# Decoder layer with retention and top-256 sparse attention: a 272-key threshold read from the smallest end, 784 keys counted on another engine, shorter mask passes, retention outputs kept in PSUM

## The chip, the cores and the metric

The program runs on one core of one Trainium2 chip. The metric is the device time of one execution in microseconds (us), taken as the median of several runs. Beside the runs there is one profiled execution, whose trace gives every instruction's start and length on the five queues of the core: TensorE (PE, with its weight loads listed as PEld), VectorE (DVE), ScalarE (ACT), GpSimd (POOL) and SyncE (SP), which issues the DMAs.

## The reference, cut to what matters

One decoder layer on 1024 tokens with 16 meta tokens in front (so 1040 keys at most), model width 1024. Two token mixers work side by side on the same normed input; their outputs are joined, projected, and an MLP follows.

```
# A) retention: 4 heads of 128, in chunks of 128 tokens, state S carried from chunk to chunk
scores  = (q_c k_c^T) * decay_mask           # within the chunk
o       = scores v_c + (q_c * xi) S          # xi = exp(log_gamma*(i+1)) per row i and head
y_ret   = silu(g) * rmsnorm(o, gain)         # norm over the head's 128 columns, EPS 1e-6

# B) sparse attention: per query an index score for every causal key, the best 256 kept
score   = sum_h iw_h * relu(iq_h . ik)       # NEG where not causal
_, sel  = lax.top_k(score, 256)              # ties: the lower key index first
p       = softmax(q . k[sel] + t5_bias)      # 8 heads of 64, one shared k and v
y_dsa   = p v[sel]

h = h + concat(y_ret, y_dsa) @ w_out
h = h + square(relu(rmsnorm(h) @ w_ff1)) @ w_ff2
```

The kernel does not gather. For each block of 128 queries it finds the 256th largest score of every row, makes a row of 0 and 1e30 from it (0 for a kept key) and adds that to the logits.

## The kernel before, in words

The 1024 queries are 8 tiles of 128; query tile i sees `ncol[i]` = 16 + 128(i+1) keys, so 144, 272, 400, 528, 656, 784, 912 and 1040. Tile 0 needs no choice (144 keys are fewer than 256). Large products run as three passes in float32r: each operand is split into a rounded high half (ACT) and a remainder (POOL or DVE).

The stages follow one another on TensorE, with the other engines' work for the next stage laid between:

1. The first norm and the index: for each tile, small projections, the index queries (`index_q`) and the index scores (`index`: two matmuls per head and key range, a Relu on ACT, a multiply-add on DVE into `sc[i]`).
2. The query projection of the attention (tensor `qn`), then retention. For each of 4 heads: `ret_meta` (the 16 meta tokens give the first state), then 8 chunks, 32 chunks in all. `ret_in` projects one chunk into one PSUM buffer of 128x512 (24 matmuls of 512 columns) and reads q, k, v and the gate out of it: DVE multiplies by cos and sin (`t`, lines 437 and 438), ACT makes `vz` and `th`, DVE `gs` and `fg`. Three such buffers (`psA`) exist, so TensorE can be at most three projections ahead. `ret_out`, one chunk later, transposes q and k, forms scores `sm` (DVE), the output `p2` (PE) and the next state `S` (DVE). ACT copies the output scaled by the row factor into `oh` (line 501) and squares it with a sum (line 502). After every fourth chunk DVE multiplies `oh` by the norm's factor and `fg` (line 506), and a DMA stores it to `yrd`.
3. The threshold search `topk` belongs to no TensorE stage: it runs on DVE and ACT while TensorE does stages 1 and 2. It is a bisection over the 31 bits of the float's pattern, a round per bit. Tiles 2, 3, 4 and 5 (400, 528, 656, 784 keys) are one group: DVE counts the scores at or above the candidate in one pass per tile (line 713), then two small instructions give the next candidate. Tiles 1, 6 and 7 (272, 912, 1040 keys) are the other: ACT counts with a Sign activation and a sum (line 718), DVE turns each tile's count into a bit (line 744) and makes the next candidate (line 752), on which ACT's next round waits. Then each tile's mask is made by DVE (lines 771 to 779): a count of greater scores, the places of equal ones, a running sum over these, two combining passes and a last one that writes `sc[i]`.
4. Attention: units of one query tile and four heads (`attend_p`, `attend_v`), mixed with the output projection (`out_piece`, whose weights `load_cols` splits on ACT, POOL and DVE).
5. Second norm, MLP in a Strassen-like form; from 725 us on.

The SBUF of stages 1 to 3 (pool `p1`, named `big`) is given back as a whole before stage 4's pool `p2` takes the same bytes. The tile `pm` (the probabilities of the meta keys) is allotted in `p2` and set to zero by DVE (line 795) before its first use; so that memset waits for the last user of the bytes it takes, among them the store of the last `oh`.

The order of the instructions on each engine is not written out: a scheduler places them, before the program runs, by its own estimate of times. On the chip every engine then works through its own list in that order, and waits where an operand isn't ready.

Of the kernel before, what the change touches and what calls it, by code (L numbers as in the profile page):

```python
# [12 lines left out]
I32 = mybir.dt.int32  # L13
# [23 lines left out]
def shape_constants():  # L37
# [44 lines left out]
def layer(ctx, tc, x, meta, norm1_w, w_in, ret_w, q_w, k_w, rel, w_out, norm2_w, w1, w2,  # L82
# [52 lines left out]
    for f in (1.0, 4.0, 64.0):  # L135
# [3 lines left out]
    def rsqrt(ms, k, f=1.0, P=128):  # L139
        y = small.tile([128, k], F32, name="rs_y", tag=f"rsy{k}", bufs=1 if k == 9 else 6)  # L140
        nc.gpsimd.tensor_tensor(y[:P], ms, epst[f][:P, :k], op=ALU.add)
# [43 lines left out]
    def split(raw, n, alt=False):  # L185
# [3 lines left out]
        nc.scalar.activation(shp, raw, AF.Copy)  # L189
        if alt:  # L190
            altc[0] += 1
        (nc.vector if alt and altc[0] % 2 else nc.gpsimd).tensor_tensor(shl, raw, shp.bitcast(F32), op=ALU.subtract)  # L192
        return hi, lo

    def load_cols(src, slices, d0=0, nd=8, alt=False):
        n = sum(w for _, w in slices)
        hs, ls = [], []
        for d in range(d0, d0 + nd, 2):
# [14 lines left out]
            for j in range(2):  # L213
                h, l = split(raw[:, j], n, alt)
# [203 lines left out]
    bias = ap_.tile([128, 8, WIN], F32, name="bias")  # L418
    kr = rsqrt(kss, 9)
# [41 lines left out]
    def ret_in(h, c):  # L461
        hs, ls = st["w", h]
        q = c % 4
        if q == 0:
            st["ss", h] = small.tile([128, 4], F32, name="ssr")
            st["oh", h] = big.tile([128, 4, 128], F32, name="oh", tag="oh", bufs=3)
# [8 lines left out]
        gs = big.tile([128, 128], F32, name="gs", tag="gs", bufs=2)  # L475
        nc.vector.tensor_tensor(gs, ps[:, 384:512], rgain[:, 128 * h:128 * h + 128], op=ALU.mult)  # L476
        nc.vector.scalar_tensor_tensor(st["fg", h][:, q], th, 1.0, gs, op0=ALU.add, op1=ALU.mult)
        return h, c, ro, vz, st["ss", h], st["oh", h], st["fg", h]

    def ret_out(h, c, ro, vz, ssr, oh, fg):  # L480
# [13 lines left out]
        p2 = psB()  # L494
        nc.tensor.matmul(p2[:, 0:128], qkT[:, 0:128], S, start=True, stop=False)
        nc.tensor.matmul(p2[:, 0:128], sm, vz, start=False, stop=True)
# [4 lines left out]
        nc.scalar.activation(oh[:, q], p2[:, 0:128], AF.Copy, scale=vecs[:, 0, h:h + 1])  # L501
        nc.scalar.activation(jk, oh[:, q], AF.Square, scale=2.0 * 128.0 ** -0.5, accum_out=ssr[:, q:q + 1])
        if q == 3:
            r = rsqrt(ssr, 4, 4.0)
            for j in range(4):
                nc.vector.scalar_tensor_tensor(oh[:, j], oh[:, j], r[:, j:j + 1], fg[:, j], op0=ALU.mult, op1=ALU.mult)
# [85 lines left out]
    def attend_v(i, g):  # L592
# [6 lines left out]
        for k, (b, k0, kp) in enumerate(tiles):  # L599
# [8 lines left out]
            if b == 8:  # L608
                ph, pl = at["pm"], at["pm"][ML:]
# [46 lines left out]
    def out_w(ch, alt=False):  # L656
        ow[0] = load_cols(w_out, [(512 * ch, 512)], alt=alt)
# [62 lines left out]

    def topk(g, on_act):
# [451 lines left out]
```

## Time and profile before

| what | us |
|---|---|
| median of 3 runs (1337.89 to 1338.53) | 1338.28 |
| the profiled execution's own time | 1337.21 |
| its span, first to last instruction | 1335.4 |
| PE busy in the span | 1260.4 (94%) |
| DVE busy | 1080.1 (81%) |
| ACT busy | 752.5 (56%) |
| POOL busy | 264.7 (20%) |

The span is cut below at the points where the work changes. "chunks" are retention's; a chunk's end is the end of its projection on PE.

| stretch, us | work on PE | PE busy | DVE busy |
|---|---|---|---|
| 106 to 189 | index tiles 5 to 7, query projection, chunk 1 | 81.52 of 83.00 | 79.67 |
| 189 to 285.7 | chunks 2 to 14 | 89.56 of 96.70 | 93.58 |
| 285.7 to 386.8 | chunks 15 to 27 | 93.46 of 101.10 | 92.50 |
| 386.8 to 438.5 | chunks 28 to 32, first attention unit | 46.08 of 51.70 | 46.49 |
| 438.5 to 453 | the seam into attention | 6.08 of 14.50 | 6.94 |
| 453 to 725 | attention, output projection, second norm | 251.14 of 272.00 | 207.13 |

How to read it: a stretch's length is what counts for the time. A matmul's busy time reaches beyond the start of the next one, since they are pipelined, so PE busy is not what PE needs; the need is the number of matmuls times the distance of their starts where nothing waits. DVE's and ACT's rows overlap a little too (some 80 ns).

### The profile page before, as it was taken

What the parts mean: (1) busy time and instruction counts of PE and PEld (TensorE: products, weight loads), DVE (VectorE), ACT (ScalarE), POOL (GpSimd) and SP (SyncE); (2) the same over time, 40 slices, a digit from 0 to 9 for tenths busy, and PEclk for the clock granted to TensorE, in tenths of its full rate; (3) what the DMA queues carried; (4) which work ended last, traced back from release to release, by engine and by line L of the source; (5) the groups of instructions that cost most, each with busy time, mean ns of one, the idle gap of its engine ahead of it and who ended that gap; (6) DMA issues with size and microseconds to landing.
All of it is one profiled execution on the core that took longest, in us unless ns stands there. A gap on an engine that the chain in (4) does not pass through costs nothing. (4 is left out here: it accounts for less than half of the span.)

```text
span 1335.4 us, 18540 instructions
## 1 busy us (share of the span) xinstructions
PE 1260.4 (94%) x6144; PEld 1044.1 (78%) x6144; DVE 1080.1 (81%) x2395; ACT 752.5 (56%) x1598; POOL 264.7 (20%) x305
## 2 busy tenths in 40 slices
PE   5999999899898699899997999999999999999998
PEld 5888877688687577787775888888887888888887
DVE  5579999999978778677659878777778988887875
ACT  6566657787644567666656545445556444444442
POOL 4003471433526323410244000000000200000000
PEclk8999999899899799999998999999999999999999
DMA  8103040211202111212263444434537844435222
GB/s 276 61 17 90 32 124 17 71 36 50 59 25 71 64 59 37 71 49 79 100 208 103 139 145 144 159 131 151 188 110 286 349 183 159 158 127 189 95 88 102
DMA packets 93664, 153.73 MB, mean 115 GB/s; under 512 B 7240, under 2 KB 47344, under 8 KB 89856
## 3 DMA queue, kind: packets, MB, share of 16 engines
q1 hardware_dynamic: 93568, 152.56, 33.1%
q8 instruction: 48, 0.79, 0.2%
q14 instruction: 48, 0.39, 0.1%
HBM read 110.58 MB, written 43.46 MB: 115 GB/s over the span
## 5 line engine op out<-in xcount | busy, mean ns | idle before, releaser
L924 ACT ACTIVATE wh<-ga 128x512 fp32r<-128x512 f32 x144 | 87.2, 628 | 158.1 <-PE psB L1072 141.4
L242 PE MATMUL psA<-wh,uh 128*128 128x512 f32 x376 | 152.2, 405 | 3.6 <-DVE gs L476 2.0
L243 PE MATMUL psA<-wh,ul 128*128 128x512 f32 x376 | 150.1, 400 | 0.0
L244 PE MATMUL psA<-wl,uh 128*128 128x512 f32 x376 | 149.9, 399 | 0.0
L925 DVE TENSOR_TENSOR wl<-ga,wh 128x512 fp32r<-128x512 f32 x144 | 96.7, 688 | 47.3 <-ACT wh L924 46.8
L924 ACT ACTIVATE wh<-sum 128x512 fp32r<-128x512 f32 x128 | 78.5, 625 | 77.3 <-DVE sum L921 71.2
L1072 PE MATMUL psB<-wh,wl 128*128 128x512 f32 x280 | 109.1, 389 | 0.2 <-DVE wl L925 0.2
L1073 PE MATMUL psB<-wl,wh 128*128 128x512 f32 x280 | 108.9, 389 | 0.0
L1071 PE MATMUL psB<-wh 128*128 128x512 f32 x280 | 106.8, 389 | 0.0
L718 ACT ACTIVATE jk_top<-sc,tcand 128x272 bf16<-128x272 f32 (+2 forms) x93 | 84.9, 913 | 32.0 <-DVE tcand L752 29.9
L713 DVE TENSOR_SCALAR_CACHE_REDUCE jk_cnt<-sc,tcand 128x400 bf16<-128x400 f32 (+1 forms) x124 | 102.1, 823 | 0.8
L925 DVE TENSOR_TENSOR wl<-sum,wh 128x512 fp32r<-128x512 f32 x128 | 87.7, 685 | 5.9 <-ACT wh L924 5.9
L991 POOL COPY ga<-wl 128x1 f32<-128x1 f32 x8 | 6.6, 829 | 404.8 <-DVE wl L925 361.1
L242 PEld LDWEIGHTS psA<-wh,uh 128*128 128x128 f32 x376 | 72.0, 192 | 17.8 <-DVE gs L476 2.6
L244 PEld LDWEIGHTS psA<-wl,uh 128*128 128x128 f32 x376 | 71.9, 191 | 14.7
L243 PEld LDWEIGHTS psA<-wh,ul 128*128 128x128 f32 x376 | 72.2, 192 | 13.1
L192 POOL TENSOR_TENSOR wl<-wr,wh 128x512 fp32r<-128x512 f32 x56 | 78.2, 1413 | 20.3 <-ACT wh L189 13.2
L354 ACT ACTIVATE rl<-psB,absw 128x320 f32<-128x320 f32 (+5 forms) x104 | 52.7, 555 | 33.6 <-PE psB L352 19.9
L611 DVE TENSOR_TENSOR ph<-psB,ph 128x512 fp32r<-128x512 f32 x72 | 49.2, 687 | 20.4 <-ACT ph L610 15.6
L1072 PE MATMUL psA<-wh,wl 128*128 128x512 f32 x168 | 65.4, 389 | 0.0
L1073 PE MATMUL psA<-wl,wh 128*128 128x512 f32 x168 | 65.4, 389 | 0.0
L1071 PE MATMUL psA<-wh 128*128 128x512 f32 x168 | 64.9, 389 | 0.0
(375 smaller groups left out, 3658.2 us busy)
## 6 DMA issues: line engine op xcount, KB each, us to landing
ga<-hid SPq DMA_DIRECT2D x28, 1024.0 KB, 4.9
wr<-in_w_ff_dram SPq DMA_DIRECT2D x34, 512.0 KB, 4.7
hid<-hs SPq DMA_DIRECT2D x48, 256.0 KB, 2.0
wr<-in_w_in_dram SPq DMA_DIRECT2D x32, 256.0 KB, 3.1
gb<-in_w_ff_dram SPq DMA_DIRECT2D x8, 1024.0 KB, 5.0
ga<-in_w_ff_dram SPq DMA_DIRECT2D x8, 1024.0 KB, 5.8
wr<-in_w_out_dram SPq DMA_DIRECT2D x12, 512.0 KB, 4.0
xt<-in_x_dram SPq DMA_DIRECT2D x8, 512.0 KB, 4.5
```

The source lines that it names most:

```text
L192: (nc.vector if alt and altc[0] % 2 else nc.gpsimd).tensor_tensor(shl, raw, shp.bitcast(F32), op=ALU.subtract)
L242: nc.tensor.matmul(ps[:P, :n], uh, wh, start=d == 0, stop=False)
L243: nc.tensor.matmul(ps[:P, :n], ul, wh, start=False, stop=False)
L244: nc.tensor.matmul(ps[:P, :n], uh, wl, start=False, stop=d == 7)
L354: nc.scalar.activation(r[:, :w], ps[:, :w], AF.Relu, scale=absw[:, i, h:h + 1])
L713: nc.vector.tensor_scalar(jk_[:, :ncol[i]], sc[i], cand[:, j:j + 1], 0.0, op0=ALU.is_ge, op1=ALU.add, accum_out=cnt[:, j:j + 1])
L718: nc.scalar.activation(jk_top[:, :ncol[i]], sc[i], AF.Sign, scale=-1.0, bias=cand[:, j:j + 1], accum_out=cnt[:, j:j + 1])
L924: nc.scalar.activation(view(hi), s, AF.Copy)
L925: nc.vector.tensor_tensor(view(lo), s, view(hi).bitcast(F32), op=SUB)
L1071: nc.tensor.matmul(ps[tb], ah[:, t], bh, start=j == 0 and m not in CONT, stop=False, skip_group_check=True)
L1072: nc.tensor.matmul(ps[tb], al[:, t], bh, start=False, stop=False, skip_group_check=True)
L1073: nc.tensor.matmul(ps[tb], ah[:, t], bl, start=False, stop=j == NO - 1, skip_group_check=True)
```

## The change

- `topk`'s group on DVE loses the 784-key tile and keeps 400, 528 and 656; the group on ACT gets it and loses the 272-key tile: 784, 912, 1040. The bits of ACT's group are made for all three tiles at once (against a row of limits `tlim`), and the part of the next candidate that doesn't need the count (`tflip`) is made beforehand.
- The 272-key tile has a routine of its own, `top_few`: the 256th largest of 272 is the 17th smallest, so the scores are negated (ACT), DVE takes the largest eight three times, striking them out twice, and picks one.
- `masks` replaces the passes after the search: ACT counts with Sign, DVE marks the equal scores and counts them in one pass, the running sum and the two combining passes stay on DVE, and ACT writes the last one.
- Retention: the four outputs of a group of chunks stay in one PSUM buffer `p2` (one of the five `psB`); ACT squares them from there and no longer copies them; the row factor moves into the EPS of the norm. The norm's weight `rgain` is no longer multiplied into the gate (`gs` is gone, `fg` reads PSUM) but into the rows of `w_out` that belong to retention: `split` scales ACT's half and takes the remainder with one scalar_tensor_tensor on DVE.
- `pm` is allotted in the attention pool, beside `bias`, and set to zero by POOL early in retention.

The core of the diff:

```
     def split(raw, n, alt=False, gain=None):
-        nc.scalar.activation(shp, raw, AF.Copy)
+        nc.scalar.activation(shp, raw, AF.Copy, scale=1.0 if gain is None else gain)
...
+        else:
+            nc.vector.scalar_tensor_tensor(shl, raw, gain, shp.bitcast(F32), op0=ALU.mult, op1=ALU.subtract)
...
+    pm = ap_.tile([128, 512], F32R, name="pm")
+    nc.gpsimd.memset(pm.bitcast(F32), 0.0)
...
+            st["p2", h] = psB()
...
-        nc.vector.tensor_tensor(gs, ps[:, 384:512], rgain[:, 128 * h:128 * h + 128], op=ALU.mult)
-        nc.vector.scalar_tensor_tensor(st["fg", h][:, q], th, 1.0, gs, op0=ALU.add, op1=ALU.mult)
+        nc.vector.scalar_tensor_tensor(st["fg", h][:, q], th, 1.0, ps[:, 384:512], op0=ALU.add, op1=ALU.mult)
...
-        nc.scalar.activation(oh[:, q], p2[:, 0:128], AF.Copy, scale=vecs[:, 0, h:h + 1])
-        nc.scalar.activation(jk, oh[:, q], AF.Square, scale=2.0 * 128.0 ** -0.5, accum_out=ssr[:, q:q + 1])
+        nc.scalar.activation(jk, po, AF.Square, scale=2.0 * 128.0 ** -0.5, accum_out=ssr[:, q:q + 1])
...
+    def masks(i, T, jk_):
+        nc.scalar.activation(jk_[:, :n], sc[i], AF.Sign, scale=-1.0, bias=T, accum_out=cnt[:, 0:1])
+        nc.vector.tensor_scalar(eq[:, :n], sc[i], T, 0.0, op0=ALU.is_equal, op1=ALU.add, accum_out=cnt[:, 1:2])
...
+        nc.vector.tensor_tensor_scan(cum[:, :n], eq[:, :n], eq[:, :n], 0.0, op0=ALU.add, op1=ALU.max)
+        nc.vector.scalar_tensor_tensor(eq[:, :n], cum[:, :n], need, eq[:, :n], op0=ALU.is_gt, op1=ALU.mult)
+        nc.vector.scalar_tensor_tensor(eq[:, :n], sc[i], T, eq[:, :n], op0=ALU.is_lt, op1=ALU.add)
+        nc.scalar.activation(sc[i], eq[:, :n], AF.Copy, scale=BIG)
...
+    def top_few(i):
+        k = n - TOPK
+        nc.scalar.activation(neg, sc[i], AF.Copy, scale=-1.0)
+        for t in range(k // 8 + 1):
+            nc.vector.max(out=m8, in_=neg)
+            if t < k // 8:
+                nc.vector.match_replace(out=neg, in_to_replace=m8, in_values=neg, imm_value=-3e38)
...
-    runs = [topk([2, 3, 4, 5], False), topk([1, 6, 7], True)]
+    runs = [top_few(1), topk([2, 3, 4], False), topk([5, 6, 7], True)]
...
-    at["pm"] = p2["p"].tile([128, 512], F32R, name="pm")
-    nc.vector.memset(at["pm"].bitcast(F32), 0.0)
```

The order changes with it. Three places matter, all on DVE.

First, index tile 5. The rows begin with the zero count of the 656-key tile (`tz`); `iq` is the index query, `sc` with `rl` the index scores, `wl` the remainder of a weight. Before:

```order
L713 TENSOR_SCALAR jk_cnt,tcnt<-sc,tz 128x656
L342 TENSOR_TENSOR iq<-psB,iq 64x4x128
L192 TENSOR_TENSOR wl<-wr,wh 128x512 x2
L278 COPY kn<-smp 128x64
L284 TENSOR_SCALAR w_119<-smp 128x8
L285 SCALAR_TENSOR_TENSOR absw<-w_119 128x8
L356 TENSOR_SCALAR sc<-rl,sgnw 128x384
```

And now:

```order
L718 TENSOR_SCALAR jk_cnt,tcnt<-sc,tz 128x656
L772 TENSOR_SCALAR tt<-tcnt 128x3
L346 TENSOR_TENSOR iq<-psB,iq 64x4x128
L780 TENSOR_SCALAR tcand<-tt 128x3
L194 TENSOR_TENSOR wl<-wr,wh 128x512
L718 TENSOR_SCALAR jk_cnt,tcnt<-sc,tcand 128x400
L194 TENSOR_TENSOR wl<-wr,wh 128x512
L718 TENSOR_SCALAR jk_cnt,tcnt<-sc,tcand 128x528
L282 COPY kn<-smp 128x64
L288 TENSOR_SCALAR w_117<-smp 128x8
L360 TENSOR_SCALAR sc<-rl,sgnw 128x384
L718 TENSOR_SCALAR jk_cnt,tcnt<-sc,tcand 128x656
```

The group no longer waits for tile 5, so its rounds begin here: 12 rounds of three counts stand ahead of retention's first chunk, where 6 rounds of four (and one count) stood.

Second, chunk 18, from the reading of its projection (`t`) to that of chunk 19. Before:

```order
L437 TENSOR_TENSOR t_3261<-psA,pk 128x256
L438 TENSOR_TENSOR t_3262<-psA,pk 128x256
L744 TENSOR_SCALAR tt<-tcnt 128x1
L713 TENSOR_SCALAR jk_cnt,tcnt<-sc,tcand 128x784
L752 SCALAR_TENSOR_TENSOR tcand<-tcand,tt 128x3
L748 TENSOR_SCALAR tt<-tcnt 128x4
L752 SCALAR_TENSOR_TENSOR tcand<-tcand,tt 128x4
L713 TENSOR_SCALAR jk_cnt,tcnt<-sc,tcand 128x400
L744 TENSOR_SCALAR tt<-tcnt 128x1
```

And now:

```order
L443 TENSOR_TENSOR t_3260<-psA,pk 128x256
L444 TENSOR_TENSOR t_3261<-psA,pk 128x256
L793 SCALAR_TENSOR_TENSOR tcand<-tt,tflip 128x3
L790 TENSOR_SCALAR tflip<-tcand 128x3
L791 TENSOR_TENSOR tt<-tcnt,tlim 128x3
L793 SCALAR_TENSOR_TENSOR tcand<-tt,tflip 128x3
L790 TENSOR_SCALAR tflip<-tcand 128x3
L481 SCALAR_TENSOR_TENSOR fg<-th,psA 128x128
```

DVE's counts ended in chunk 12 and its group's masks in chunk 15; up to chunk 26 only the small instructions of ACT's rounds are left beside retention's own.

Third, the seam, where the last `oh` of retention meets the first `pm`. Before:

```order
L583 TENSOR_REDUCE m_5169<-mn 128x1
L506 SCALAR_TENSOR_TENSOR oh<-oh,rs_y,fg 128x128 x4
L795 MEMSET pm 128x512
L611 TENSOR_TENSOR pm<-psB,pm 16x512 x2
L577 ISA P,mn<-psA,sc 128x32
```

And now:

```order
L592 RECIPROCAL rs<-sums 128x4
L616 TENSOR_TENSOR pm<-psB,pm 16x512
L588 TENSOR_REDUCE m_4968<-mn 128x1
L582 ISA P,mn<-psA,mb 128x240
L582 ISA mn 128x1
L560 TENSOR_TENSOR qs<-psA,qs 64x4x128
L582 ISA P,mn<-psA,sc 128x32
```

The memset is gone from DVE's list and the first `pm` stands ahead of the last `oh`.

## Rows read from the trace of the kernel before

**Rows 1.** Stretches: length, busy us (instructions) per engine, granted clock, DMA share, GB/s.

```profile
60.00:106.00 46.00, 45.11 (x274) 39.01 (x272) 31.99 (x74) 30.95 (x78) 1.56 (x5) 1.00 0.06 19
106.00:189.00 83.00, 81.52 (x392) 68.56 (x391) 79.67 (x156) 51.70 (x101) 44.28 (x39) 0.98 0.26 81
189.00:285.70 96.70, 89.56 (x449) 74.37 (x448) 93.58 (x312) 68.31 (x177) 31.25 (x50) 0.96 0.17 49
285.70:386.80 101.10, 93.46 (x471) 77.38 (x470) 92.50 (x297) 73.60 (x198) 41.35 (x60) 0.95 0.18 50
386.80:438.50 51.70, 46.08 (x254) 39.06 (x253) 46.49 (x125) 23.54 (x83) 29.27 (x32) 0.97 0.21 67
438.50:453.00 14.50, 6.08 (x28) 4.80 (x28) 6.94 (x21) 3.99 (x10) 2.75 (x2) 0.53 0.17 55
...
750.00:800.00 50.00, 50.00 (x222) 41.40 (x221) 39.27 (x64) 25.69 (x47) 0.00 (x0) 1.00 0.48 169
```

**Rows 2.** Timeline of PE at 404 us: start, length, line, tiles, count.

```profile
404.44 0.39 PE L489 MATMUL psB<-qkT 128*128 128x128 f32 x2
404.66 0.39 PE L491 MATMUL psB<-vz,ro 128*128 128x128 f32 x2
```

**Rows 3.** Waits of PE, 195 to 440 us: total, times, longest.

```profile
PE psB L496 <- DVE sm L493: 12.0, 4, 5.1
```

**Rows 4.** Waits of ACT, 195 to 390 us.

```profile
ACT jk_top L718 <- DVE tcand L752: 29.9, 21, 5.2
```

**Rows 5.** Timelines of PE and DVE around chunk 1.

```profile
196.95 0.41 DVE L437 TENSOR_TENSOR t<-psA,pk 128x256 f32<-128x256 f32 x1
...
198.16 1.28 DVE L713 TENSOR_SCALAR_CACHE_REDUCE jk_top<-sc,tz 128x1040 bf16<-128x1040 f32 x1
...
199.38 2.77 DVE L294 SCALAR_TENSOR_TENSOR knl<-psB,knh 64x512 fp32r<-64x512 f32 x4
...
203.30 0.47 PE L242 MATMUL psA<-wh,uh 128*128 128x512 f32 x1 [1.62 <-DVE tt L732]
```

**Rows 6.** DVE's groups by shape, 100 to 440 us: busy us, mean ns, idle.

```profile
L713 DVE TENSOR_SCALAR_CACHE_REDUCE jk_cnt<-sc,tcand 128x784 bf16<-128x784 f32 x31 | 31.7, 1023 | 0.1
L713 DVE TENSOR_SCALAR_CACHE_REDUCE jk_cnt<-sc,tcand 128x656 bf16<-128x656 f32 x31 | 27.6, 889 | 0.0
L713 DVE TENSOR_SCALAR_CACHE_REDUCE jk_cnt<-sc,tcand 128x528 bf16<-128x528 f32 x31 | 23.5, 757 | 0.2
L713 DVE TENSOR_SCALAR_CACHE_REDUCE jk_cnt<-sc,tcand 128x400 bf16<-128x400 f32 x31 | 19.3, 624 | 0.5
L476 DVE TENSOR_TENSOR gs<-psA,rgain 128x128 f32<-128x128 f32 x32 | 9.0, 283 | 1.0 <-ACT th L474 0.8
L499 DVE SCALAR_TENSOR_TENSOR S<-S,psB 128x128 f32<-128x128 f32 x28 | 7.7, 275 | 0.0
L771 DVE TENSOR_SCALAR_CACHE_REDUCE jk_top<-sc,tfin 128x272 bf16<-128x272 f32 x1 | 0.5, 496 | 0.3 <-POOL tfin L764 0.3
```

**Rows 7.** The tile `oh` on DVE, 189 to 440 us: min/median/max ns.

```profile
L506 DVE SCALAR_TENSOR_TENSOR oh<-oh,rs_y,fg x29: 340/348/2271, 238.4 to 439.1; 128x128 f32<-128x128 f32 x29
```

**Rows 8.** ACT's groups by shape, 100 to 440 us.

```profile
L718 ACT ACTIVATE jk_top<-sc,tcand 128x1040 bf16<-128x1040 f32 x31 | 36.0, 1163 | 0.6
L718 ACT ACTIVATE jk_top<-sc,tcand 128x912 bf16<-128x912 f32 x31 | 32.7, 1054 | 0.6
...
L718 ACT ACTIVATE jk_top<-sc,tcand 128x272 bf16<-128x272 f32 x31 | 16.2, 523 | 30.8 <-DVE tcand L752 29.9 <-DVE tcand L737 0.7
...
L501 ACT ACTIVATE oh<-psB,pk 128x128 f32<-128x128 f32 x32 | 11.6, 362 | 23.9 <-PE psB L496 23.6
```

**Rows 9.** The seam: DVE's timeline from 439 us, and PE's waits, 438 to 453.

```profile
439.13 3.06 DVE L506 SCALAR_TENSOR_TENSOR oh<-oh,rs_y,fg 128x128 f32<-128x128 f32 x4
444.60 0.48 DVE L795 MEMSET pm<- 128x512 f32 x1 [2.41 <-issue]
...
PE psB L612 <- DVE pm L611: 8.4, 2, 7.0
```

More of the change, by code (lines that the diff above doesn't have):

```diff
@@ L134, in layer @@
     epst = {}
-    for f in (1.0, 4.0, 64.0):
+    for f in (1.0, 64.0):
         epst[f] = const.tile([128, 9], F32, name=f"eps{int(f)}")
@@ L139, in rsqrt @@
     def rsqrt(ms, k, f=1.0, P=128):
-        y = small.tile([128, k], F32, name="rs_y", tag=f"rsy{k}", bufs=1 if k == 9 else 6)
-        nc.gpsimd.tensor_tensor(y[:P], ms, epst[f][:P, :k], op=ALU.add)
+        y = small.tile([128, k], F32, name="rs_y", tag=f"rsy{k}", bufs=1 if k == 9 else 4)
+        nc.gpsimd.tensor_tensor(y[:P], ms, epst[f][:P, :k] if isinstance(f, float) else f, op=ALU.add)
         nc.gpsimd.tensor_tensor(y[:P], y[:P], nhalf[:P, :k], op=ALU.pow)
@@ L213, in load_cols @@
             for j in range(2):
-                h, l = split(raw[:, j], n, alt)
+                h, l = split(raw[:, j], n, alt, gain[:, d + j:d + j + 1] if gain is not None and d + j < 4 else None)
                 hs.append(h)
@@ L407, in layer @@
     nc.sync.dma_start(qgain, bcast(q_w, 64))
-    shift(const, 288)
-    rgain = big.tile([128, 512], F32, name="rgain")
-    nc.sync.dma_start(rgain, bcast(ret_w, 512))
+    shift(const, 320)
+    rgain = const.tile([128, 4], F32, name="rgain")
+    nc.sync.dma_start(rgain, bass.AP(tensor=ret_w.tensor, offset=ret_w.offset, ap=[[1, 128], [128, 4]]))
     att = ExitStack()
@@ L493, in ret_out @@
         nc.vector.tensor_tensor(sm, p1[:, 0:128], decT[:, h], op=ALU.mult)
-        p2 = psB()
-        nc.tensor.matmul(p2[:, 0:128], qkT[:, 0:128], S, start=True, stop=False)
-        nc.tensor.matmul(p2[:, 0:128], sm, vz, start=False, stop=True)
+        po = p2[:, 128 * q:128 * q + 128]
+        nc.tensor.matmul(po, qkT[:, 0:128], S, start=True, stop=False)
+        nc.tensor.matmul(po, sm, vz, start=False, stop=True)
         if c < 7:
@@ L656, in out_w @@
     def out_w(ch, alt=False):
-        ow[0] = load_cols(w_out, [(512 * ch, 512)], alt=alt)
+        ow[0] = load_cols(w_out, [(512 * ch, 512)], alt=alt, gain=rgain)
     def out_mm(ch, b, ys, hp):
@@ L732, in topk @@
         nc.vector.tensor_scalar(t0, cnt, TOPK - 0.5, -1.0, op0=ALU.is_ge, op1=ALU.add)
-        step = st("tstep", I32, 1)
         if on_act:
+            step = st("tstep", I32, 1)
             nc.vector.tensor_scalar(step, t0, 2.0, 1.0, op0=ALU.mult, op1=ALU.add)
+            lim = st("tlim", F32, 1)
+            for j, i in enumerate(g):
+                nc.vector.memset(lim[:, j:j + 1], ncol[i] - 2.0 * TOPK + 1.5)
         cand = st("tcand", I32)
@@ L767, in topk @@
         for j, i in enumerate(g):
[L768 to L784 removed]
+            masks(i, thr[:, j:j + 1], jk_)
+    runs = [top_few(1), topk([2, 3, 4], False), topk([5, 6, 7], True)]
     while runs:
```

78 lines of the change are left out of this document (43 added, 35 removed).

## The prediction

> **What bounds the kernel now.** I read the busy times by stretch first. [rows 1] PE looks busy throughout, so the question is what PE needs. At 750 us, where it never waits, 222 matmuls of 512 columns take 50.00 us: 0.225 us each [rows 1]. Two of 128 columns start 0.22 us apart from the next pair: 0.11 us each [rows 2]. With these prices:
>
> - 189 to 285.7 us, 13 chunks: 13 x 24 = 312 large matmuls, 70.2 us, and 449 - 312 = 137 small ones, 15.1 us; 85.3 of 96.7 us, so 11.4 us over the need.
> - 285.7 to 386.8: 70.2 + 159 x 0.11 = 87.7 of 101.1; 13.4 over.
> - 386.8 to 438.5: 5 chunks, 27.0 + 134 x 0.11 = 41.7 of 51.7; 10.0 over.
> [...]
>
> [...] In the first two of these stretches DVE is busy 93.58 of 96.70 and 92.50 of 101.10 us, so DVE sets the pace there; the waits of PE say the same, the largest being for `sm`, which DVE makes: 12.0 us in four waits [rows 3]. At the seam PE waits 8.4 us for `pm`, 7.0 of it at once, behind a memset that itself stood 2.41 us idle after four `oh` instructions of 3.06 us [rows 9].
>
> **The counts that leave DVE.** 31 counts of 784 keys at 1.023 us are 31.7 us, `gs` 9.0 us [rows 6]. Both lie in the stretches that DVE bounds. The four `oh` of the seam took 765 ns each against a median of 348 and a longest of 2271 [rows 7, 9]; over 32 that is between 0 and 32 x 0.417 = 13.3 us, and I take 9, most of it from the disturbed ones. The 93 small bits become 31: a few us at most. What this frees is some 50 us of DVE, more than PE can use, so the sum goes by PE's excess and by where DVE's work now stands.
>
> **The front-load.** 12 rounds of three counts now stand ahead of chunk 1: a round is 0.624 + 0.757 + 0.889 = 2.27 us, 27.2 in all. Six rounds of four (3.29) and one count of 0.62 stood there: 20.4 [rows 6]. That is +6.8 us on a DVE that was already busy 79.67 of 83.00 us [rows 1]. Six more rounds bring 12 small instructions, bounded by nothing and by 0.275 us each (the `S` row), so 0 to 3.3; I take 2. The count of zero for 1040 keys (1.28) and two of the four `knl` (half of 2.77) move from behind chunk 1's reading to ahead of it [rows 5], which delays the reading by 2.7 us and shortens the way from it to the release of the buffer: counts of 400 and 528 keys stood on that way too (about 6 us) and stand behind it now, beside chunk 2's `t`, so I put it at 3.2 us. Net: the release that PE waited for at 203.30 us (1.62 us [rows 5]) comes 6.8 + 2 + 2.7 - 2.9 = about 9 us later (8 to 12), and PE stands for that.
>
> From there to chunk 13 DVE does less: 19 rounds of 2.27 (43.1 us) and the first mask passes (3.5) where 15 rounds of 3.29 stood (49.3), 13 `gs` less (3.7), the `oh` of three groups (about 4), bits (1): about 11 us. DVE stays behind PE all the while, so these come off the path one to one, and the delay is paid back by chunk 14. **Term: 0 us** in 106 to 285.7 (from +6, if DVE's counts are still the pace and half of the saving falls into waits for PE, to -6, if DVE had slack enough ahead of chunk 1).
>
> **Chunks 15 to 27.** DVE's counts end in chunk 12 and the group's masks in chunk 15. Here ten rounds of four stood before (32.9 us) beside 3.7 of `gs`: of 92.5 us DVE keeps some 55 of 101. PE would come near its need, 13.4 us less, but for ScalarE. ACT's counts of 1040 and 912 keys are 1.163 and 1.054 us, so 784 take about 0.945; the 272 take 0.523 [rows 8]: +0.42 us a round. ACT is busy 73.60 us here; 16 rounds more by 0.42 is +6.7, 13 copies at 0.362 less is -4.7 [rows 1, 8], so 75.6; a hop to DVE and back in each round costs what ACT now waits for, 29.9 us over 31 rounds [rows 4], nearly 1 us, or 15 us here if it stays. That is 91 us of chain beside a PE need of 87.7. So PE isn't quite free: **term: -11 us** (-6 if the hops stay as long and ACT's order is tight, -14 if they shrink to what the two small instructions cost).
>
> **Chunks 28 to 32.** DVE is busy 46.49 of 51.70 us here, on the masks of 912 and 1040 keys. They lose two passes to ACT, which has only 23.54 us of work [rows 1], but the merged pass is dearer than a plain compare, 784's mask comes in as well, and some `wl` moves from POOL to DVE. I count DVE's work as nearly the same. **Term: -1 us** (-5 to +3).
>
> **The seam.** The memset goes to POOL long before, and the first `pm` no longer stands behind the last `oh` and its store. The 8.4 us on `pm` [rows 9] go; what is late next is the softmax of the first unit, with the masks ahead of it on DVE. **Term: -9 us** (-5 to -11.2).
>
> **The rest.** `top_few` adds six passes over 272 keys, at 0.496 us (nearest row) to 1.02 us each (784 keys) [rows 6]: 3 to 6 us of DVE, and the mask of that tile, both in or before 60 to 106 us or the start of the next stretch, where DVE is busy 31.99 of 46.00 and PE 45.11 [rows 1], so PE hides them; without this cover they would be paid in full. Eight remainders of `w_out` move from POOL to DVE, at 0.69 us (a quarter of 2.77 [rows 5]) 5.5 us, in attention, where DVE has 65 us idle in 272. A retention group holds one of the five `psB` for four chunks, in place of one per chunk: three or four are left for the transposes and scores, of which a chunk uses two. **Term: 0** (-2 to +2).
>
> Sum: 0 - 11 - 1 - 9 + 0 = -21 us. The profiled execution took 1337.21 us and the median is 1.07 above, so 1338.3 - 21 = **1317 us**.
>
> [...] Reading PSUM in place of SBUF on DVE: the `S` update, which reads PSUM, takes 275 ns and `gs`, which reads it too, 283, below the 348 of `oh` from SBUF at the same size [rows 6, 7]. [...]
>
> The slow `oh`: the same instruction takes 340 ns at one time and 2271 at another [rows 7]. [...]
>
> **The rivals.**
> B, *a relief that doesn't come*: either the front-load is paid in full (+9, DVE's saving in chunks 2 to 13 falling into waits), or the seam stays since the first `pm` finds another late operand (+9). [...] Against: DVE never waits in these chunks, so less work shows. 1317 + 9 = **1326 us**.
> C, *full relief*: DVE absorbs the front-load, 189 to 285.7 gains half of its excess (-6), chunks 15 to 27 nearly all (-13), 28 to 32 3, the seam all 11.2: -33, **1305 us**. Against: ACT's chain above.
> D, *ScalarE takes DVE's place*: its counts grow by 31 x 0.42 = 13 us and its mask passes by about 12 (two passes over seven tiles, at the Sign rows' price), and it loses 32 copies, 9 us with their overlap: +16 us. If each round's chain paces the chunks, that comes onto the path, less 9 at the seam: **1345 us**, slower. It decides once a round with its hop is longer than PE's share of it: the hop would have to stay above 1 us although DVE is emptier. Against: ACT waited 23.9 us ahead of its copies, nearly all for PE [rows 8].
> E, *no change to speak of*: half of D against the seam, 1338 us.
>
> **How the numbers follow.** A 0.60 with its own range of 1308 to 1326 (the terms' bounds, not all at one end); B 0.17; C 0.10; D 0.08; E 0.05. Leaving out D, E and some tails at the bottom, the range is 1303 to 1330. A measurement of this kernel can tell about 0.2%, 2.7 us. Faster 0.87, same 0.05, slower 0.08.
>
> **What would show it.** In the profile after: PE's wait of 1.62 us near 203 us grown to about 10, with DVE full up to chunk 12; DVE well below 65% in chunks 15 to 27 and the 12.0 us of PE on `sm` mostly gone; ACT's waits for `tcand` a round; 512-column projections following each other at 6.4 to 6.8 us a chunk; no wait for `pm` at the seam. I am wrong if PE still waits for DVE after chunk 15, if ACT's rounds last 6.5 us or more there, or if the seam keeps a wait of 5 us under another name.

## The result, and the profile after

The changed kernel takes 1322.01 us (median of 4 runs, 1321.96 to 1322.28) where the kernel before took 1338.40 (4 runs): 0.9877 of it, 95% interval 0.9860 to 0.9894, or 16.4 us faster. The forecast was 1317 in a range of 1303 to 1330, so direction and range hold; 16.4 of the 21 us came. The profiled execution of the changed kernel took 1322.03 us, its span is 1320.3 (before: 1335.4).

The page's first part, busy time and share of each engine, after:

```profile
PE 1254.5 (95%) x6144; PEld 1036.8 (79%) x6144; DVE 1038.5 (79%) x2277; ACT 767.3 (58%) x1588; POOL 253.5 (19%) x298
```

DVE is busy for 41.6 us less than before, ACT for 14.8 us more. The stretches after, cut at the same points of the work as in [rows 1] (first index tile 5 to chunk 1, then chunks 2 to 14, 15 to 27, 28 to 32), with the same columns:

```profile
106.00:194.90 88.90, 84.75 (x392) 69.33 (x391) 88.15 (x189) 52.55 (x104) 44.98 (x39) 0.94 0.25 75
194.90:289.20 94.30, 89.78 (x452) 74.83 (x450) 88.66 (x307) 73.07 (x176) 31.24 (x51) 0.98 0.17 51
289.20:382.70 93.50, 90.21 (x465) 74.42 (x463) 46.77 (x142) 78.37 (x185) 39.93 (x59) 1.00 0.19 54
382.70:434.00 51.30, 46.63 (x260) 38.70 (x258) 45.73 (x118) 28.29 (x85) 25.84 (x28) 1.00 0.21 68
```

The third row answers to 285.7 to 386.8 us before: DVE fell from 92.50 to 46.77 us there, a half of the stretch, and yet the stretch is shorter by 7.6 us only. The first row answers to 106 to 189: it grew by 5.9 us. PE's waits from chunk 2 to the seam (total us, times, longest), against [rows 3]:

```profile
PE psB L493 <- ACT qkT L491: 3.3, 4, 1.6
PE psB L499 <- ACT jk L505: 2.7, 2, 2.4
PE psA L246 <- DVE fg L481: 2.2, 4, 1.2
PE psB L500 <- DVE sm L497: 1.5, 1, 1.5
```

The 12.0 us of waits for `sm` are down to 1.5. A wait that wasn't there before is the second line: the matmul of an output waits for ACT's square of the output before it, with which it now shares a PSUM buffer. The two largest waits are now for ACT, 6.0 us together.

The table follows one instruction through both traces: the start of the last matmul of a chunk's projection (line 244 before, 248 now), then the first product of a probability with the values, the first matmul of the MLP and the span's end. "late" is the time after less the time before.

| point | before, us | after, us | late |
|---|---|---|---|
| chunk 1 | 188.5 | 194.3 | +5.9 |
| chunk 4 | 209.5 | 212.3 | +2.8 |
| chunk 6 | 222.7 | 231.3 | +8.6 |
| chunk 8 | 236.8 | 244.6 | +7.9 |
| chunk 9 | 253.3 | 254.1 | +0.8 |
| chunk 14 | 285.3 | 288.8 | +3.5 |
| chunk 24 | 355.6 | 361.2 | +5.6 |
| chunk 25 | 375.0 | 370.5 | -4.5 |
| chunk 27 | 386.4 | 382.3 | -4.1 |
| chunk 32 | 429.6 | 423.7 | -5.9 |
| first value product | 446.6 | 431.9 | -14.7 |
| MLP | 705.7 | 688.2 | -17.5 |
| end | 1335.4 | 1320.3 | -15.1 |

Here lies the answer to most that follows. The gain isn't spread over the chunks that DVE was to have held up. It stands at three places: 7.1 us between chunks 8 and 9, 10.1 us between 24 and 25, and 8.8 us at the seam. The first two are the changes to the second and to the fourth head; the change to the third, from chunk 16 to 17, takes 11.4 us before and 11.6 after. Between such places the changed kernel loses more than it wins. Of the 5.9 us that it is late at chunk 1, 3.1 are back by chunk 4; then 5.8 are lost by chunk 6, and 4.8 between chunks 9 and 24.

The loss at chunk 6, on PE and, ahead of it, on ACT:

```profile
222.36 0.58 PE L499 MATMUL psB<-S,qkT 128*128 128x128 f32 x2 [2.39 <-ACT jk L505]
```

```profile
218.54 0.95 ACT L723 ACTIVATE jk_top<-sc,tcand 128x784 bf16<-128x784 f32 x1 [1.79 <-DVE tcand L793]
```

Three counts of ACT (784, 912 and 1040 keys) stand ahead of the square that PE waits for, and behind the wait the granted clock is 0.56 from 222.3 to 226.2 us. The square alone isn't the cause: with ACT's copy back and with the squares late (both below), where PE doesn't wait for it here, chunks 4 to 6 lose 5.5 and 5.4 us. All the kernels below in which DVE's rounds begin as early as in the change lose 3.9 to 6.2 us there against the kernel before, the others 0.1 to 1.6; how the early start leads to it wasn't followed.

### The profile page after: what moved, and what is told of

It reads as the page before. It is cut to its first block, busy times and chain, and to the rows that moved or that the text cites. A ratio compares the mean times of both kernels' runs of the same rounds, so it can differ in the third digit from the quotient of the medians.

```text
span 1320.3 us, 18430 instructions
## 1 busy us (share of the span) xinstructions
PE 1254.5 (95%) x6144; PEld 1036.8 (79%) x6144; DVE 1038.5 (79%) x2277; ACT 767.3 (58%) x1588; POOL 253.5 (19%) x298
## 5 line engine op out<-in xcount | busy, mean ns | idle before, releaser
L723 ACT ACTIVATE jk_top<-sc,tcand 128x784 bf16<-128x784 f32 (+2 forms) x93 | 98.3, 1057 | 23.9 <-DVE tcand L793 19.8
L247 PEld LDWEIGHTS psA<-wh,ul 128*128 128x128 f32 x376 | 71.4, 190 | 12.2
L718 DVE TENSOR_SCALAR_CACHE_REDUCE jk_cnt<-sc,tcand 128x400 bf16<-128x400 f32 (+2 forms) x93 | 70.3, 756 | 1.0
L194 POOL TENSOR_TENSOR wl<-wr,wh 128x512 fp32r<-128x512 f32 x48 | 67.0, 1418 | 18.4 <-ACT wh L189 12.3
L952 DVE TENSOR_TENSOR sum<-wr,wr 128x512 f32<-128x512 f32 x48 | 31.7, 686 | 41.5 <-DMA wr<-in_w_ff_dram 36.0
```

What stands on the lines that cost most here:

```text
L194: e.tensor_tensor(shl, raw, shp.bitcast(F32), op=ALU.subtract)
L247: nc.tensor.matmul(ps[:P, :n], ul, wh, start=False, stop=False)
L718: nc.vector.tensor_scalar(jk_[:, :ncol[i]], sc[i], cand[:, j:j + 1], 0.0, op0=ALU.is_ge, op1=ALU.add, accum_out=cnt[:, j:j + 1])
L723: nc.scalar.activation(jk_top[:, :ncol[i]], sc[i], AF.Sign, scale=-1.0, bias=cand[:, j:j + 1], accum_out=cnt[:, j:j + 1])
L952: nc.vector.tensor_tensor(s, *srcs, op=op)
```

## What happened at the head changes

DVE's timeline of the kernel before, at the second head (start, length, line, count):

```profile
238.43 5.25 DVE L506 SCALAR_TENSOR_TENSOR oh<-oh,rs_y,fg 128x128 f32<-128x128 f32 x4
243.60 0.15 DVE L752 SCALAR_TENSOR_TENSOR tcand<-tcand,tt 128x4 int32<-128x4 int32 x1
243.68 0.28 DVE L493 TENSOR_TENSOR sm<-psB,pk 128x128 f32<-128x128 f32 x1
```

PE at that time, with what it waited for:

```profile
244.01 0.79 PE L496 MATMUL psB<-vz,sm 128*128 128x128 f32 x2 [5.06 <-DVE sm L493]
```

And POOL, which was making the remainders of the next head's weights:

```profile
237.20 6.33 POOL L192 TENSOR_TENSOR wl<-wr,wh 128x512 fp32r<-128x512 f32 x5
```

Four `oh` instructions of 0.35 us took 5.25 us, and `sm`, for which PE stood 5.06 us, was queued behind them. In steps of 1.3 us, each `oh` ended 0.15 us after one of POOL's subtractions. At the fourth head the same four took 4.61 us from 355.14 us on. At the third they took 0.35 us each from 308.8 us on: POOL's last subtraction had ended at 306.0, so whether the two meet hangs on the order and on timing. The kernel after, DVE at the second head:

```profile
239.96 1.12 DVE L510 SCALAR_TENSOR_TENSOR oh<-psB,rs_y,fg 128x128 f32<-128x128 f32 x4
241.00 0.80 DVE L791 TENSOR_TENSOR tt<-tcnt,tlim 128x3 int32<-128x3 f32 x1
```

with POOL at its subtractions as before:

```profile
240.48 2.54 POOL L194 TENSOR_TENSOR wl<-wr,wh 128x512 fp32r<-128x512 f32 x2
```

The last two `oh` ran beside POOL's subtraction at full speed (at most 0.351 us, below); the next instruction, which reads two tiles in SBUF, took 0.80 us (its median is 0.163) and ended at 241.80 us, as POOL's first subtraction did (at about 241.8). At the third and the fourth head of this kernel the four `oh` had ended before POOL's first subtraction (at the fourth, at 357.2 and 357.6 us), so there it is the order that kept them apart. All 32 `oh` of the kernel after (minimum, median, longest), against [rows 7]:

```profile
L510 DVE SCALAR_TENSOR_TENSOR oh<-psB,rs_y,fg x32: 332/340/351, 240.0 to 434.4; 128x128 f32<-128x128 f32 x32
```

The long wait of PE at the fourth head cost more than its length. The kernel before around the fourth head, by stretches (columns of [rows 1]; the granted clock is the third number from the end):

```profile
350.00:358.00 8.00, 7.90 (x46) 6.58 (x44) 8.00 (x17) 7.47 (x18) 6.91 (x7) 1.00 0.14 35
358.00:366.00 8.00, 1.71 (x7) 0.95 (x7) 8.00 (x16) 3.49 (x12) 7.07 (x8) 0.65 0.66 198
366.00:372.00 6.00, 6.00 (x17) 4.75 (x18) 6.00 (x11) 3.42 (x9) 1.77 (x2) 0.61 0.26 87
372.00:378.00 6.00, 6.00 (x35) 4.87 (x33) 4.89 (x14) 3.29 (x7) 0.53 (x3) 1.00 0.00 0
```

PE was idle for most of 358 to 366 us; then it worked without a wait but at a granted clock of 0.61 (0.50 from 366 to 370 us): 17 matmuls in 6.00 us, nearly all of 512 columns, where 0.225 us each [rows 1] would let 26 start. That is some 2 us on top of the wait, an estimate from these counts. After the change the granted clock is 1.00 from 289 to 434 us.

## The experiments

Each time stands against runs of the kernel before on the same chip, whose medians were 1339.55 to 1340.44; the intervals reach 1.4 to 3.7 us to either side. Every edit also makes the scheduler place the other instructions anew, so an order changes a little with each of them. The removal of `gs`, `top_few` and the joint bits of ACT's group were not tried alone.

The steps at the three head changes, from the last matmul of one chunk's projection to that of the next (us, from each kernel's profiled execution), show where each of the kernels below wins or loses:

| kernel | chunk 8 to 9 | 16 to 17 | 24 to 25 |
|---|---|---|---|
| before | 16.5 | 11.4 | 19.4 |
| the change | 9.4 | 11.6 | 9.3 |
| outputs in PSUM alone | 14.3 | 10.2 | 15.1 |
| the change without them | 16.3 | 15.8 | 12.1 |
| POOL that doesn't read | 9.2 | 11.0 | 12.2 |
| the change, old masks | 9.8 | 16.8 | 9.0 |
| the change, late group | 12.1 | 9.9 | 9.0 |
| the change, 784 keys on DVE | 15.1 | 10.7 | 15.8 |

### One part alone: the outputs in PSUM

In the kernel before (the row factor moves into the EPS as well):

```
+            st["p2", h] = psB()                      # one buffer for four chunks
...
-        nc.scalar.activation(oh[:, q], p2[:, 0:128], AF.Copy, scale=vecs[:, 0, h:h + 1])
-        nc.scalar.activation(jk, oh[:, q], AF.Square, ...)
+        nc.scalar.activation(jk, po, AF.Square, ...)
...
-                nc.vector.scalar_tensor_tensor(oh[:, j], oh[:, j], r[:, j:j + 1], fg[:, j], ...)
+                nc.vector.scalar_tensor_tensor(oh[:, j], p2[:, 128 * j:128 * j + 128], r[:, j:j + 1], fg[:, j], ...)
```

> The kernel before with one part alone: the four outputs of a group stay in one PSUM buffer, the row factor goes into the EPS, oh is made from PSUM; the counts, the masks, gs and pm as before. New theory: the two long stalls of PE before the change, at the second and at the fourth head (5.3 us near 239 us and 6.6 near 359 to 366), come from four oh instructions of 1.35 us each beside POOL's remainders of the next head's weights, and the one PSUM operand takes the collision away: 8 to 10 us less, 1328 to 1331, all oh at about 0.34 us, DVE as full as before. Rival, the prediction's own: the 31.7 us of counts were what held PE, so this alone gives 3 us at most, 1335 or more.

1334.43 us, 6.0 under before (ratio 0.9954, 0.9940 to 0.9968); 5.5 us early at chunk 27, with every count and mask still on DVE. All `oh` took 0.335 to 0.352 us, and here the four of the fourth head stand in the middle of POOL's subtractions:

```profile
352.95 1.11 DVE L506 SCALAR_TENSOR_TENSOR oh<-psB,rs_y,fg 128x128 f32<-128x128 f32 x4
```

```profile
351.24 7.56 POOL L192 TENSOR_TENSOR wl<-wr,wh 128x512 fp32r<-128x512 f32 x5
```

The gain is short of the 8 expected. PE now waits 4.0 us for ACT's squares, 3.5 of them at the second and the fourth head; whether it would be faster without these waits wasn't tried in this kernel. But the gain is twice what the rival allowed. ACT's 32 copies went too (11.6 us of ACT [rows 8]); the kernel in which POOL doesn't read, below, keeps them and gains more, so they needn't go for the stalls to go.

### That part undone

The changed kernel with ACT's copy back and `oh` made from SBUF.

> The changed kernel with that part undone: ACT copies each output to SBUF again and oh is made from there. New theory: oh takes up to 1.4 us again wherever POOL makes remainders, and the second and fourth head begin with stalls of 4 to 5 us: 1328 to 1331. Rival: with the counts gone DVE has room in the later chunks, only the first of the two stalls returns, and ACT's 32 copies cost nothing: 1322 to 1326.

1337.33 us, 3.1 under before (0.9975, 0.9965 to 0.9986): of the 16.4 us 13 are gone, more than either theory expected. `oh` in this kernel:

```profile
L510 DVE SCALAR_TENSOR_TENSOR oh<-oh,rs_y,fg x32: 339/353/1709, 241.6 to 453.0; 128x128 f32<-128x128 f32 x32
```

Chunk 9 comes 8.4 us late and chunk 17 13.3 us late, though DVE does the fewer counts of the changed kernel: now the third head collides too. At the fourth the step is 12.1 us where it was 19.4 before, so 7.3 of the 10.1 us that the change wins there come without the outputs in PSUM. In sum the rest of the change gives nothing up to the seam without them: at chunk 32 it is 7.2 us behind the kernel before.

### POOL that doesn't read

The kernel before, with POOL writing zeros into the remainders of the second to fourth retention head's weights:

```
-        (...).tensor_tensor(shl, raw, shp.bitcast(F32), op=ALU.subtract)
+        if blank[0]:                                  # weights of retention heads 2 to 4
+            nc.gpsimd.memset(shl.bitcast(F32), 0.0)
+        else:
+            (...).tensor_tensor(shl, raw, shp.bitcast(F32), op=ALU.subtract)
```

> The kernel before, but for the second to fourth retention head POOL doesn't subtract the rounded half from the weight: it writes zeros into wl, reading nothing (the remainders of these heads' weights are left out of the computation). New theory: it is POOL reading SBUF that stretches DVE's oh to 1.35 us, so with POOL only writing all oh at the head changes take about 0.35 us, the two long stalls of PE (near 239 and 359 us) go, and the kernel is 6 to 10 us faster than before, as with the outputs in PSUM or somewhat better since the masks aren't stretched either. Rival: oh is slow there because DVE is full or because of the tile it reads; then oh stays at 1.3 us beside POOL and the time within 3 us of before.

1327.71 us, 11.8 under before (0.9909, 0.9887 to 0.9931). Chunk 27 is 12.9 us early, with 124 counts, all masks and `gs` on DVE, and `oh` in SBUF. POOL and DVE of this kernel at the second head:

```profile
236.30 2.39 POOL L194 MEMSET wl<- 128x512 f32 x5
```

```profile
236.95 1.13 DVE L510 SCALAR_TENSOR_TENSOR oh<-oh,rs_y,fg 128x128 f32<-128x128 f32 x4
```

The four `oh` are at full speed beside POOL's writes. Three long ones are left, 1.51, 1.51 and 2.29 us (from 385.7 us on and at the seam); each stands beside a `mb<-bias,sc` of POOL, which reads and takes 1.47, 1.48 and 2.20 us, so the length of an `oh` goes with that of POOL's instruction. The four of the second head ran within an unbroken row of POOL's writes and weren't held, so it isn't POOL's being busy that holds them. POOL's writes are shorter than its subtractions as well (0.5 for 1.3 us); how much of the 11.8 us comes from that isn't told apart. That POOL's subtractions cause the stalls is shown: without them the steps at the second and the fourth head took 9.2 and 12.2 us where they took 16.5 and 19.4.

### The seam

`pm` back in the pool that takes the freed bytes, set to zero by DVE:

```
-    pm = ap_.tile([128, 512], F32R, name="pm")
-    nc.gpsimd.memset(pm.bitcast(F32), 0.0)
+    at["pm"] = p2["p"].tile([128, 512], F32R, name="pm")
+    nc.vector.memset(at["pm"].bitcast(F32), 0.0)
```

> The changed kernel with one part undone: pm is allotted in the pool that takes the freed bytes again and set to zero by DVE there. Theory: the seam gives 9 of the 16 us, so about 1331 us, the loss all within the seam, with PE waiting some 8 us for pm. Rival: DVE now reaches the seam so early that the memset's wait hides behind other work: within 2 us of 1322.

1333.62 us, 6.1 under before (0.9952, 0.9936 to 0.9968), so about 10 us of the 16.4 are gone. PE waits 4.9 us for `pm` at the seam. From chunk 32 to the first value product this kernel wins 2.5 us where the change wins 8.8. But the loss isn't all within the seam, as was expected: the first value product is 10.0 us early where it was 14.7, the MLP 6.2 where it was 17.5, so more than half of the difference arises in attention, which wasn't followed further.

> The kernel before with two parts alone, the PSUM outputs and pm in the attention pool set to zero by POOL (gs in one buffer and four of a small tile in place of six, for room). New theory: these two hold the whole gain of the change, 1318 to 1322, though every count and mask is as before. Rival, the prediction's own: about 1338 - 9 - 3 = 1326 or more, since the counts are still on DVE.

Both parts in the kernel before: 1328.21 us, 12.2 under (0.9908, 0.9893 to 0.9923), less than the 18 to 22 of the new theory and near the rival's number, but not for the rival's reason: chunk 27 is 7.7 us early with all counts on DVE, and from chunk 32 to the first value product 7.0 are won (8.8 in the change). So these two alone give three quarters of the gain.

### The masks

> The changed kernel with the old passes of the masks, all on DVE. Theory: DVE has idle time from chunk 15 on (13.99 us busy of 36 in chunks 18 to 23) and the masks of 784 to 1040 stand in chunks 28 to 32, where DVE is nearly full: 0 to 3 us more, 1322 to 1325. Rival: the two ACT passes a tile stand before vz, th and qkT on a full ACT, and taking them away gives 2 us or more, 1320 or less.

The changed kernel with the old passes, all on DVE: 1331.31 us, 9.1 under before (0.9940, 0.9919 to 0.9962): 7 us gone by the medians, 4 by the start of the MLP. Both expectations were too low. DVE of this kernel at the third head:

```profile
301.76 1.73 DVE L736 SCALAR_TENSOR_TENSOR eq<-cum,need,eq 128x656 bf16<-128x656 f32 x1
303.41 1.23 DVE L789 TENSOR_TENSOR tt<-tcnt,tlim 128x3 int32<-128x3 f32 x1
304.56 1.98 DVE L737 SCALAR_TENSOR_TENSOR eq<-sc,tcand,eq 128x656 bf16<-128x656 f32 x1
306.47 1.21 DVE L791 SCALAR_TENSOR_TENSOR tcand<-tt,tflip 128x3 int32<-128x3 int32 x1
307.61 0.49 DVE L738 TENSOR_SCALAR sc<-eq 128x656 f32<-128x656 bf16 x1
308.02 1.23 DVE L788 TENSOR_SCALAR tflip<-tcand 128x3 int32<-128x3 int32 x1
309.16 0.28 DVE L497 TENSOR_TENSOR sm<-psB,pk 128x128 f32<-128x128 f32 x1
```

and PE:

```profile
309.49 0.80 PE L500 MATMUL psB<-vz,sm 128*128 128x128 f32 x2 [4.40 <-DVE sm L497]
```

The same collision at other instructions: POOL subtracts from 301.50 to 309.22 us, and instructions of three elements a row take 1.2 us. In the change the two passes over 656 keys meet this burst as well (300.28 and 303.37 us, 2.00 and 1.98 us), but `sm` stands right behind them and PE waits 1.5 us. Here three more instructions stand ahead of `sm`, and chunk 17 is 9.8 us late, where the change is 3.7.

### The front-load, and the 784 keys

DVE's group made to start with the 784-key tile, as it did before the change (the zero threshold is made from that tile's scores):

```
-        nc.vector.memset(zero, 0.0)
+        if on_act:
+            nc.vector.memset(zero, 0.0)
+        else:
+            nc.vector.tensor_scalar(zero, sc[5][:, ncol[5] - k:], 7e30, None, op0=ALU.is_equal)
```

> The changed kernel with the DVE group's first count made to depend on the 784-key tile's scores, so that its rounds start where they started before the change. Theory: the 5.9 us by which chunk 1 is later go, and since DVE's counts then last to about chunk 16 instead of 12 part of it is paid there: 2 to 4 us less, 1318 to 1320. Rival one: the counts only move and cost the same wherever they stand: 1322 within 2. Rival two: the front-load was worth it, since DVE had slack there: 1325 or more.

1317.10 us, 22.6 under before (0.9831, 0.9816 to 0.9846), a little better than expected. Chunk 1 is 1.0 us late in place of 5.9, chunk 24 2.9 early in place of 5.6 late. At the MLP the two kernels are 6.1 us apart, so what the front-load costs is never paid back. Where it is paid first shows in the changed kernel's stretch ahead of chunk 1's end:

```profile
174.00:195.00 21.00, 17.39 (x74) 12.40 (x72) 21.00 (x30) 11.74 (x24) 16.41 (x13) 0.76 0.44 125
```

DVE is busy throughout, PE starts 74 matmuls in 21 us, and its granted clock is 0.76; before, the stretch from 174 us to chunk 1's end took 15 us (64 matmuls, granted clock 0.89).

The other way to lose the front-load is to give the 784 keys back:

```
-    runs = [top_few(1), topk([2, 3, 4], False), topk([5, 6, 7], True)]
+    runs = [top_few(1), topk([2, 3, 4, 5], False), topk([6, 7], True)]
```

> The changed kernel with the 784-key tile back in DVE's group (400, 528, 656, 784) and ACT's group 912 and 1040 alone; all else as changed. Theory: DVE paces chunks 1 to about 22 again, so of the 7.6 us of chunks 15 to 27 most go, about 1328 to 1331; the front-load goes too (4 us back): net 1324 to 1328. Rival: ACT paces, and with 0.95 us less in a round it frees more than DVE loses: 1318 or less.

1317.31 us, 22.4 under before (0.9835, 0.9821 to 0.9850): not the theory's time but the rival's, 1318 or less, though not for the rival's reason, since the late group takes as long with the 784 keys on ACT. Beside the late group, on the same chip, this is the test of the 784 keys alone: on ACT 1317.10, on DVE 1317.31. 31.7 us of DVE's work moved to ACT are worth nothing in sum. The way there differs: at chunk 25 the late group is 8.6 us ahead, at chunk 32 only 2.4, at the MLP 1.8. In the late group the two mask passes over 656 keys stand at 313.83 and 314.75 us, clear of POOL's subtractions, and take 0.9 us each; with the 784 keys on DVE they meet POOL's burst at the fourth head, and a stall is left:

```profile
353.48 1.70 DVE L738 SCALAR_TENSOR_TENSOR eq<-cum,need,eq 128x656 bf16<-128x656 f32 x1
355.10 1.23 DVE L791 TENSOR_TENSOR tt<-tcnt,tlim 128x2 int32<-128x2 f32 x1
356.25 1.98 DVE L739 SCALAR_TENSOR_TENSOR eq<-sc,tcand,eq 128x656 bf16<-128x656 f32 x1
358.16 1.22 DVE L793 SCALAR_TENSOR_TENSOR tcand<-tt,tcand 128x2 int32<-128x2 int32 x1
```

Four instructions beside POOL again, and PE waited 3.5 us for `sm`.

> The changed kernel with the 656-key tile on ACT and the 784-key tile on DVE: DVE counts 400, 528, 784, ACT 656, 912, 1040. DVE's rounds then wait for the 784-key tile by themselves (no front-load), ACT's round is 0.1 us shorter, DVE's 0.13 longer. Theory: as the late group, 21 to 24 us under before. Rival: the late group's gain came from its order and not from the front-load: 16 to 18 under before, like the change.

DVE 400, 528, 784, ACT 656, 912, 1040: 1319.57 us, 20.0 under before (0.9843, 0.9816 to 0.9871), between the two expectations, with runs from 1314.8 to 1322.1; it doesn't decide. Chunk 1 is 1.3 us early, so the front-load is gone here too, and PE waits 5.9 us for `qkT`, from ACT.

### The new coupling

> The changed kernel with ACT's four squares of a group issued after the group's fourth output in place of one after each output. Theory: keeping four outputs in one PSUM buffer made each output's matmul wait for the square of the output before it (five waits of PE's weight loads, 6.4 us, in the trace of the changed kernel), and ACT does that square behind its counts; without it 3 to 6 us less, 1316 to 1319, and no wait of that matmul for the square within a group. Rival: the matmul waits for the next thing ACT makes anyway (qkT, vz): within 2 us of 1322.

The four squares of a group issued after its last output: 1321.43 us, 18.3 under before (0.9861, 0.9846 to 0.9877), not told apart from the change. PE's waits for the squares (2.7 us) are gone; those for `fg` grew from 2.2 to 3.2 us, and 2.1 us for POOL's `wl` came. The rival's time holds: PE waits for something else that is as late, though not for ACT alone.

### Away from the collisions

> The late group once more (DVE's rounds start with the 784-key tile), and the remainders of the third and fourth retention head's weights are made by DVE in place of POOL: 16 x 0.7 = 11 us more for DVE in chunks 9 to 24, and no POOL reading there. Theory: mask passes and the small instructions of ACT's rounds are stretched to 1.2 to 2 us beside POOL in the changed kernel too; without that 1 to 3 us less than the late group (22.6 us under before), so 23 to 26 under before. Rival: DVE's 11 us cost more than the collisions, at most 20 under before.

> The kernel with the 784-key tile on DVE (keys784_on_dve), and the remainders of the fourth retention head's weights made by DVE in place of POOL. There the four instructions of DVE ahead of the fourth head (two mask passes over 656 keys and two small ones) took 1.70, 1.23, 1.98 and 1.22 us beside POOL's remainders, and PE stood 3.8 us. Theory: without POOL's reading they take 0.9 and 0.16 us, the 3.8 us go, DVE pays 8 x 0.7 us where it waits for nobody: 2 to 4 us better than keys784_on_dve, 24 to 27 under before. Rival: the eight remainders on DVE delay sm as much as POOL did, 20 to 23 under before.

The edit in both is `dve=h > 1` (third and fourth head) or `dve=h > 2` (the fourth) at the heads' `load_cols`, which puts the remainders on DVE. 1315.71 us (23.8 under, 0.9816, 0.9795 to 0.9836) and 1316.52 us (23.3 under, 0.9830, 0.9814 to 0.9847). In the second PE's 3.5 us for `sm` at the fourth head are gone and the MLP begins 23.7 us early in place of 21.8, but the step from chunk 24 to 25 still takes 15.6 us (15.8). The first lies within its theory, the second between theory and rival; in the medians neither is told apart from the kernel it was made from. Four versions, 22.4 to 23.8 us under before, beat the change by 6 to 7 us.

## Why the prediction was right, and where it was wrong

- **The need of PE** was right in the main: 34.8 us of excess were found in chunks 2 to 32 (11.4, 13.4 and 10.0), and there and at the seam the gain came, 11.8 and 8.8 us. No run shows the 11.2 us that C's sum and the bound of the seam's term take for the seam. What the traces show there is a granted clock of 0.53 and eight matmuls of 128 columns from 450.25 to 451.95 us, 0.21 us each in place of 0.11; by that price the 28 matmuls need some 6 us of the 14.5, an estimate that leaves 8.6. "DVE sets the pace there", of chunks 2 to 27, was the step that failed. A DVE that was 97% busy (93.58 of 96.70 us) held up nothing where what PE needed stood ahead of the filler in DVE's list; between the head changes PE ran at its own pace before and after (chunks 18 to 24: 45.6 us before, 47.5 after, where the prediction's prices give about 45). The excess sat in a few long stalls. The rows to see it were there: 12.0 us in only four waits, the longest 5.1 [rows 3], and an `oh` of 0.348 us that took up to 2.271 [rows 7]. The prediction read the second as DVE time to be saved (9 us) and never asked what stood behind the slow ones in DVE's list.
- **The front-load**: +9 us for chunk 1, paid back by chunk 14, was forecast; +5.9 came (6.4 from 107 us on). 3.1 were back by chunk 4, 5.8 were lost again by chunk 6, the second head's stall gave 7.1, and at chunk 14 it was 3.5. The size was near, the payback failed, for the reason above: less DVE work in chunks 2 to 14 didn't speed a PE that wasn't waiting for it. The cost showed ahead of chunk 1, where the earlier rounds did hold PE up, as the late group shows, not as a longer wait at 203 us. The term is +4.0 in place of 0, within its bounds.
- **Chunks 15 to 27**: -7.6 for -11, within the bounds and for another cause: the fourth head's stall (-10.1) and +2.5 in the rest. The outputs in PSUM alone shorten that step by 4.3 us, and the other parts without them by 7.3; the steps beside it got no shorter, though DVE had half of its work left. So that this term came near is luck in part. ACT's counts of 784 keys took what was interpolated (0.945 forecast):

```profile
L723 ACT ACTIVATE jk_top<-sc,tcand 128x784 bf16<-128x784 f32 x31 | 29.4, 949 | 22.8 <-DVE tcand L793 19.8 <-DVE tcand L780 2.4 <-DVE need L734 0.4
```

- **Chunks 28 to 32**: -1.8 for -1. **The seam**: -8.8 for -9; the wait for `pm` went as forecast; undoing that part cost 10 us, though less than half of it by the first value product. **The rest**: -0.9 for 0 (-0.5 ahead of 107 us, -2.8 in attention and the second norm, +2.4 in the MLP); `top_few`'s first five passes took 0.43 to 0.44 us each, below the lower bound, in time that PE hid.
- **The sum** of -21 was too large by the two terms that rested on DVE's pace, 4.0 and 3.4 us; the others gave 1.5 back, so the span fell 5.9 us short of it.
- **PSUM in place of SBUF**: `oh` from PSUM took 340 ns (median), from SBUF 348, so reading PSUM cost nothing here. With two SBUF operands an `oh` beside POOL's subtraction took 1.34 to 1.44 us and ended 0.15 us after it, with one of them in PSUM 0.34. It was the heart of the matter; in the prediction the two lengths of `oh` stood beside the sum and were not put onto the path.
- **Rival B** was half right: one of its two cases, a front-load that isn't paid back, came about. **C** and **D** didn't: no 16 us came onto the path from ACT, whose waits for `tcand` fell from 29.9 to 19.8 us. But the two largest waits of PE after the change are for ACT (6.0 us), the longest of them at chunk 6.

## What to carry to other kernels

Before an engine's busy share is taken for a bound, list the gaps of the engine that is to be sped up: if its excess is a handful of long stalls, look what stands in the other engine's list ahead of the instruction that ended each, and whether those took longer than their own median. Work that a scheduler uses as filler may be moved away without any gain, as here (1317.10 us with the 784 keys on ACT, 1317.31 on DVE); moving it to another place in time can cost (6.1 us at the MLP for the front-load). An instruction that at times takes several times its median (here 2.271 us for 0.348) may point to another engine: then try another memory for an operand, another order or less work on the other engine, before fewer instructions.

## What was not expected of the hardware

- Small DVE instructions were held beside POOL's subtractions just as large ones: with three elements a row they took 0.16 to 0.17 us (medians), and up to 1.25 us each beside POOL, where the mask passes over 656 keys took 1.70 to 2.00 us for 0.9.
- An instruction with one input tile in SBUF was among them (`tflip` at 308.02 us in the kernel with the old masks, 1.23 us), so two SBUF inputs were not needed for it; why wasn't tried. One such instruction was long beside POOL's writes too (`tt<-tcnt` of four elements at 238.00 us where POOL doesn't read, 0.71 us). The counts, with one input tile as well, were not: 400 and 528 keys took 0.63 and 0.76 us (0.624 and 0.757 on average before [rows 6]) amid POOL's subtractions, at 245.58 and 246.73 us of the changed kernel. Nor were DVE instructions with an operand in PSUM: `sm`, `S` and `fg` took 0.28 to 0.29 us each, at 246.13 to 246.53 us.
- After two waits of PE of 3.95 and 1.96 us the next matmuls ran at a lower granted clock: 0.50 from 366 to 370 us in the kernel before, with 0.43 us between starts of 512 columns in place of 0.225. After the 2.39 us at chunk 6 of the changed kernel the granted clock was 0.56 for 3.9 us.
